# A delta rule's diagonal blocks, zeroed margins and decay buffer, moved within an eight-head software plan

## The chip, the cores and the metric

The kernel runs on one core of a Trainium2 chip. The metric is the device time of one execution in microseconds (us). The core has a matrix engine (TensorE, PE in the profile, with its weight loads as PEld), three engines for elementwise work (VectorE, DVE; ScalarE, ACT; GpSimd, POOL) and a queue that only issues transfers (SyncE, SP). Every engine works through its own queue in order. Engines wait for each other and for DMA transfers by semaphores.

## The reference

A decoder trunk of two layers over 1024 tokens of width 1024. Each layer projects the normalised input once, runs sparse attention and a gated delta rule side by side, gates and adds both, and projects back. The change touches the delta rule alone:

```python
qkv_b = jax.nn.silu(causal_depthwise_conv(qkv_b, conv_w[layer]))      # 4 taps, zeros ahead of the first token
q_b, k_b = l2_normalize(q_b), l2_normalize(k_b)
...
q, k, v = c4(q) * (dk ** -0.5), c4(k), c4(v)                          # chunks, 8 heads of 128
beta, gc = c3(beta), jnp.cumsum(c3(g), axis=-1)
decay = jnp.exp(jnp.where(incl, gc[..., :, None] - gc[..., None, :], -jnp.inf))
lower = jnp.where(strict, jnp.einsum('bhnid,bhnjd->bhnij', kb, k) * decay, 0.0)
tmat = jnp.eye(CHUNK) + lower
u = triangular_solve(tmat, v * beta[..., None]); w = triangular_solve(tmat, kb * jnp.exp(gc)[..., None])
q_dec = q * jnp.exp(gc)[..., None]
...
def step(state, xc):
    v_new = u_c - w_c @ state
    o_c = qd_c @ state + qk_c @ v_new
    state = state * gt_c + kd_c.T @ v_new
```

## The kernel before

Activations live as 128 partitions by tokens. Every projection in float32 is three matmuls of 128 x 512 (high times high, high times low, low times high, L388), 24 for one half of a feature tile and 48 for a whole one. A layer has a token phase (index scores, keys, values, selection), a feature phase (the delta rule), and an attention phase. The program is written with a framework whose scheduler fixes the order of each engine's queue when the program is built, by priority and by when it believes that inputs will be ready.

The feature phase (`feature_phase`, L673) runs over eight heads. For each head it projects and convolves keys, queries and values (`conv`, L736: 48 matmuls each). From the second head on it then projects the output gates of the head before (`gdn_finish`, L892: 96 matmuls). So a head takes 144 matmuls at first and 240 in steady state; the last head is followed by further gate projections.

In `conv`, ScalarE copies each accumulated half into a padded row `xp` (L748) and writes the last tap into `kf`, `qf` or `vv` (L749); VectorE adds three more taps of 128 x 1024 (L755); a tanh on ScalarE (L757) and one VectorE operation (L758) finish the activation. `xp` has two buffers in turn, and its four leading columns, the zeros ahead of the first token, are written once a layer by GpSimd (L682).

Everything else of a head is put between those projection matmuls by a plan. `plan_head` (L699) enters steps with a position, counted in projection matmuls from the head's own start; `planned` (L306) emits a step when the count reaches its position, with a priority far above the projections, and with an order on TensorE behind the matmul just emitted and on ScalarE behind the last evacuation (`issue_after`). For VectorE, GpSimd and SyncE a planned step has the priority alone, so there the scheduler may set it earlier. In order of position a head's steps are:

- 80, `decays_load` (L717): GpSimd issues a 512 KB load into `H` (two buffers), masks it (L723), and issues another of 512 KB (L727) with the queries' decays, `qe`. That tile shares its one buffer, "wide", with the tile `ln` of the inverse (L926). `decays_exp` (118): ScalarE turns `H` into decays (L734), queued behind the last evacuation.
- 100 and 106, `gdn_keys`: TensorE turns the keys (L765), ScalarE squares them (L771), VectorE sums (L772), makes `kdec` (L784), and runs the reciprocal root (`rsqrt`, L130) for the norms. 138, `gdn_row`: one row of scales goes out to memory and back as `ccomp`.
- 142 and 147, `gdn_queries`: the same squares for the queries.
- 151 to 163, `gdn_products`: products of keys with keys and queries (L831), multiplied by the decays on VectorE (L833, L834).
- 163, `gdn_inverse`: VectorE multiplies `qf` by `qe` (L838), then `inverse_blocks` (L917) writes the 32 x 32 diagonal blocks out (L925), reads them back as `ln` (L928), inverts them all by 31 steps on VectorE (L938, L940), writes the result out (L944) and reads it back into `H` (L947).
- 352 to 382, `inverse_pairs` (L949): VectorE turns three of the diagonal blocks into `XF` (L956), and TensorE joins blocks to 64 and to 128 (L965 to L992).
- 390 to 544, `gdn_chunks` (L852): 23 steps of the recurrence over eight chunks (L865 to L888), the last users of the head's `H`.
- 552, `norms` (L898): mean square and reciprocal root of the outputs on VectorE, ending in L903. 562 and 568, `outputs` (L905): TensorE turns the result (L909), VectorE gates it (L910).

In steady state, seen from the head whose keys are being projected, its predecessor's pairs lie at matmul 112 and after, and the norm and outputs of the one before that at 72, 82 and 88; the query projection ends at 96.

Of the kernel before, what the change touches and what calls it, by code (L numbers as in the profile page):

```python
# [20 lines left out]
try:  # L21
# [4 lines left out]
F32 = mybir.dt.float32  # L26
# [5 lines left out]
OP = mybir.AluOpType  # L32
# [4 lines left out]
P = 128  # L37
S = 1024
# [31 lines left out]

AT_DECAYS, AT_EXP, AT_KEYS, AT_ROW, AT_QUERIES, AT_PRODUCTS, AT_VALUES, AT_PAIRS, AT_CHUNKS, AT_NORMS, AT_OUTPUTS = (
    80, 118, (100, 106), 138, (142, 147), (151, 155, 159, 163), (204, 210), 352, 390, 552, (562, 568))

STEP_PAIRS, STEP_CHUNKS = 6, 7

# [1 line left out]
def ap(t, offset, dims):  # L79
    return bass.AP(tensor=t.tensor, offset=t.offset + offset, ap=dims)  # L80
# [13 lines left out]
class Trunk:  # L94
# [207 lines left out]
    def at(self, pos, step):  # L302

        self.plan.append((pos, len(self.plan), step))
# [368 lines left out]
    def feature_phase(self, l, ht):  # L673
        nc, tc = self.nc, self.tc
        self.yb = self.dram.tile([HEADS, P, S], F32, name="yb")
        with tc.tile_pool(name="feat", bufs=1) as p, self.banks(ch=(1, 2), oc=(1, 1), more=(1, 1)):
            XF = p.tile([P, T, 64], F32, name="xf")
            nc.gpsimd.memset(XF, 0.0)

            self.xps = [p.tile([P, S + 4], F32, name=f"xp{i}") for i in range(2)]  # L680
            for a in self.xps:
                nc.gpsimd.memset(a[:, 0:4], 0.0)  # L682
            self.count, hd = 0, None
            for h in range(HEADS + 1):
                before, hd = hd, None
                if h < HEADS:
                    hd = dict(h=h, at=self.count)
                    self.plan_head(p, hd, XF)
                    for name, base, bufs in (("kf", 1024, 3), ("qf", 0, 3), ("vv", 2048, 1)):
                        self.conv(l, p, ht, hd, name, base, bufs)  # L690
                if h >= HEADS - 1:
                    i = h - HEADS + 2
                    for f in range(sum(GATES[:i]), sum(GATES[:i + 1])):
                        self.gate_a(l, ht, f)
                if before:
                    self.gdn_finish(l, p, ht, before)
            self.planned()

    def plan_head(self, p, hd, XF):  # L699

        at = lambda pos, *steps, gap=0: [self.at(hd["at"] + pos + i * gap, f) for i, f in enumerate(steps)]
        at(AT_DECAYS, lambda: self.decays_load(p, hd))
        at(AT_EXP, lambda: self.decays_exp(hd))
        for half in range(2):
            at(AT_KEYS[half], lambda half=half: self.gdn_keys(p, hd, half))
            at(AT_QUERIES[half], lambda half=half: self.gdn_queries(hd, half))
            at(AT_VALUES[half], lambda half=half: self.gdn_values(p, hd, half))
        at(AT_ROW, lambda: self.gdn_row(p, hd))
        for i, pos in enumerate(AT_PRODUCTS):
            at(pos, lambda i=i: self.gdn_products(p, hd, 2 * i))  # L710
        at(AT_PRODUCTS[-1], lambda: self.gdn_inverse(p, hd))
        pairs = self.inverse_pairs(p, hd, XF)
        at(AT_PAIRS, *[lambda: next(pairs, None)] * 6, gap=STEP_PAIRS)
        chunks = self.gdn_chunks(p, hd)
        at(AT_CHUNKS, *[lambda: next(chunks, None)] * (3 * T - 1), gap=STEP_CHUNKS)

    def decays_load(self, p, hd):  # L717


        nc, h = self.nc, hd["h"]  # L720
        E = hd["H"] = p.tile([P, T, P], F32, name="H", bufs=2)
        nc.gpsimd.dma_start(out=E, in_=ap(self.rows, h * P, [[0, P], [8 * P, T], [1, P]]))
        masked = nc.gpsimd.affine_select(E, E, pattern=[[0, T], [1, P]], compare_op=OP.is_ge, fill=MASKED, base=0,  # L723
                                         channel_multiplier=-1)
        qe = hd["qe"] = p.tile([P, 32, 32], F32, name="wide", bufs=1).rearrange("p a b -> p (a b)")
        with self.tc.issue_after(masked.ins):
            nc.gpsimd.dma_start(out=qe.rearrange("p (t c) -> p t c", c=P),  # L727
                                in_=ap(self.rows, (T * 8 + h) * P, [[0, P], [8 * P, T], [1, P]]))
# [7 lines left out]
    def conv(self, l, p, ht, hd, name, base, bufs):  # L736

        nc = self.nc
        feat = self.feat[l]
        dst = hd[name] = p.tile([P, S], F32, name=name, bufs=bufs)  # L740
        col = base + hd["h"] * P
        cw = lambda j: feat[:, 24 * j + col // P:24 * j + col // P + 1]
        self.xps.append(self.xps.pop(0))
        xp = self.xps[0]

        def evac(hs, acc):
            o = hs.start
            nc.scalar.copy(xp[:, 4 + o:516 + o], acc)  # L748
            self.act_last = nc.scalar.activation(dst[:, hs], acc, AF.Copy, scale=cw(3)).ins  # L749

        ws = self.feat_weights(self.w_in[l], C_QKVB + col)
        for half in range(2):
            self.proj_feat(ws, half, ht, evac)
        for j in range(3):
            nc.vector.scalar_tensor_tensor(dst, xp[:, 1 + j:1 + j + S], cw(j), dst, op0=OP.mult, op1=OP.add)  # L755
        th = xp[:, 4:4 + S]
        nc.scalar.activation(th, dst, AF.Tanh, scale=0.5)  # L757
        nc.vector.scalar_tensor_tensor(dst, th, 1.0, dst, op0=OP.add, op1=OP.mult)  # L758
# [76 lines left out]

    def gdn_inverse(self, p, hd):

        self.nc.vector.tensor_mul(hd["qf"], hd["qf"], hd["qe"])  # L838
        with self.tc.high_priority(offset=AHEAD - PLANNED):
            self.inverse_blocks(p, hd["H"], hd["ccomp"])  # L840

# [107 lines left out]
    def inverse_pairs(self, p, hd, XF):  # L949

        nc, nc_ = self.nc, hd["nc"]
        XT = H = hd["H"]
        for b in range(3):
            bs = slice(32 * b, 32 * b + 32)
            co = 32 if b == 1 else 0
            nc.vector.transpose(XF[bs, :, co:co + 32], XT[bs, :, bs])  # L956
        yield
        ncb = lambda sl, n: nc_[sl, :, None].to_broadcast([sl.stop - sl.start, T, n])
        y2 = p.tile([P, T, 32], F32, name="y2", bufs=1)

        pairs = [(slice(32 * b, 32 * b + 32), slice(32 * b + 32, 32 * b + 64)) for b in (0, 2)]
        py = self.bank("ch")
        for c in range(T):
            for k, m in pairs:
                nc.tensor.matmul(py[m, 32 * c:32 * c + 32], H[k, c, m], XF[k, c, 0:32], start=True, stop=True)  # L965
        for k, m in pairs:
            nc.vector.tensor_mul(y2[m], py[m, :256].rearrange("p (c i) -> p c i", c=T), ncb(m, 32))
        yield
        pz = self.bank("ch")
        for c in range(T):  # L970
            for k, m in pairs:
                nc.tensor.matmul(pz[k, 32 * c:32 * c + 32], y2[m, c], XT[m, c, m], start=True, stop=True)
        for k, m in pairs:
            nc.scalar.copy(XT[k, :, m], pz[k, :256].rearrange("p (c i) -> p c i", c=T))
        yield
        m = slice(32, 64)
        pw = self.bank("ch")
        for c in range(T):
            nc.tensor.matmul(pw[m, 32 * c:32 * c + 32], XT[m, c, m], y2[m, c], start=True, stop=True)
        nc.scalar.copy(XF[m, :, 0:32], pw[m, :256].rearrange("p (c i) -> p c i", c=T))  # L980
        yield
        k, m = slice(0, 64), slice(64, 128)
        py = self.bank("ch")
        for c in range(T):
            nc.tensor.matmul(py[m, 64 * c:64 * c + 64], H[k, c, m], XF[k, c], start=True, stop=True)
        y3 = XF
        nc.vector.tensor_mul(y3[m], py[m].rearrange("p (c i) -> p c i", c=T), ncb(m, 64))
        yield
        pz = self.bank("ch")
        for c in range(T):  # L990
            nc.tensor.matmul(pz[k, 64 * c:64 * c + 64], y3[m, c], XT[m, c, m], start=True, stop=True)
        nc.scalar.copy(XT[k, :, m], pz[k].rearrange("p (c i) -> p c i", c=T))  # L992
# [252 lines left out]
```

## Time and profile before

| What | us |
|---|---|
| three runs, median (lowest to highest) | 2746.72 (2743.76 to 2749.48) |
| the profiled execution, its own time | 2755.04 |
| its span, first to last instruction | 2753.4 |
| granted TensorE clock, mean over the span | 0.974 |

How to read it: times are us from the span's start unless marked ns. A group's line gives source line, engine, operation, what it writes and reads, shapes and count. A row of the timeline gives start, duration, engine, line, operation, tiles, shape and count, and in brackets how long the engine sat idle before it and what ended that. A row of the waits gives who waited for whom: us in total, times, longest. The feature phase runs from about 365 to 1108 us in the first layer and from about 1740 to 2464 in the second.

### The profile page before, as it was taken

To read this page: it belongs to the slowest core of one execution; us is meant where nothing else is said; L and a number is where in the kernel's file an instruction comes from. 1 tells how busy PE (TensorE), PEld (TensorE's weight loads), DVE (VectorE), ACT (ScalarE), POOL (GpSimd) and SP (SyncE) were. 2 spreads that over 40 slices of the span, in tenths; PEclk is the share of its full clock that TensorE was granted. 3 is DMA by queue.
4 is the path that set the end of the run, shared out by engine and by line. 5 is a ranking of instruction groups with operands and counts; after the bars stand their busy time and mean duration, and the time that the engine had idled before them with its cause. 6 is when DMAs were issued, how large, how long until landed. Compare 5 with 4: busy or idle time off the path is not lost.

```text
span 2753.4 us, 42170 instructions
## 1 busy us (share of the span) xinstructions
PE 2595.2 (94%) x14858; PEld 2134.8 (78%) x14858; DVE 1886.2 (69%) x5082; ACT 1348.4 (49%) x3107; POOL 135.4 (5%) x386
## 2 busy tenths in 40 slices
PE   7999989989999999999999999899999999999998
PEld 7677767777777788898786777677778777888986
DVE  6678967666676663598356779676767666637965
ACT  5579634343333332598135796333434334237962
POOL 0122000000000000000001220000000000000000
PEclk9999999998999999999999999999999999999999
DMA  3123232142333322431411232321332323234223
GB/s 120 47 66 95 81 82 57 42 79 54 63 56 69 57 60 68 153 102 47 152 53 48 65 97 80 82 66 35 84 75 46 67 60 62 64 103 132 88 83 128
DMA packets 285431, 211.35 MB, mean 77 GB/s; under 512 B 72290, under 2 KB 239268, under 8 KB 285220
## 3 DMA queue, kind: packets, MB, share of 16 engines
q1 hardware_dynamic: 280612, 191.88, 24.8%
q0 software_dynamic: 4608, 16.78, 5.0%
q8 instruction: 117, 1.92, 0.3%
q14 instruction: 94, 0.77, 0.1%
HBM read 162.19 MB, written 46.40 MB: 76 GB/s over the span
## 4 chain that ended last, share of the span: by engine, by line
PE 56%; DVE 11%; DMA 7%; issue 3%; ACT 2%; SPq 1%; POOL 0%; DVEq 0%; ACTq 0%; POOLq 0%
PE acc L388 16%; PE more L388 7%; PE acc L365 7%; PE acc L1137 4%; PE wide L1105 4%; PE tr L1128 2%; DMA H<-xscr 2%; PE out L365 2%; DVE xtmp L938 2%; DVE xc L940 2%; PE tr L831 2%; PE out L388 2%; PE tr L765 1%; DVE w_lo L148 1%; DMA wide<-rows 1%
## 5 line engine op out<-in xcount | busy, mean ns | idle before, releaser
L388 PE MATMUL acc<-lo_t,w_hi 128*128 128x512 f32 x1240 | 511.4, 412 | 0.0
L388 PE MATMUL acc<-hi_t,w_hi 128*128 128x512 f32 x1240 | 503.2, 406 | 6.8 <-DVE gate L663 6.1
L388 PE MATMUL acc<-hi_t,w_lo 128*128 128x512 f32 x1240 | 503.7, 406 | 0.0
L147 ACT CAST w_hi<-w_raw 128x512 fp32r<-128x512 f32 (+1 forms) x336 | 201.4, 602 | 417.3 <-PE acc L388 214.6
L148 DVE TENSOR_TENSOR w_lo<-w_raw,w_hi 128x512 fp32r<-128x512 f32 (+1 forms) x336 | 223.7, 669 | 219.8 <-ACT w_hi L147 190.5
L365 PE MATMUL acc<-w_hi,hi_t 128*128 128x512 f32 (+1 forms) x768 | 287.5, 375 | 15.1 <-ACT w_hi L147 10.2
L365 PE MATMUL acc<-w_lo,hi_t 128*128 128x512 f32 (+1 forms) x768 | 286.8, 374 | 2.1 <-DVE w_lo L148 2.1
L365 PE MATMUL acc<-w_hi,lo_t 128*128 128x512 f32 (+1 forms) x768 | 285.2, 371 | 0.0
L388 PEld LDWEIGHTS acc<-hi_t,w_hi 128*128 128x128 f32 x1240 | 236.3, 191 | 57.2 <-DVE gate L663 7.5
L388 PEld LDWEIGHTS acc<-lo_t,w_hi 128*128 128x128 f32 x1240 | 236.8, 191 | 47.7
L388 PEld LDWEIGHTS acc<-hi_t,w_lo 128*128 128x128 f32 x1240 | 236.8, 191 | 45.3
L596 ACT ACTIVATE t_junk<-scores,t_bits 128x640 f16<-128x640 f32 x248 | 198.9, 802 | 29.5 <-DVE t_bits L588 24.7
L388 PE MATMUL more<-lo_t,w_hi 128*128 128x512 f32 x488 | 203.0, 416 | 0.0
L388 PE MATMUL more<-hi_t,w_hi 128*128 128x512 f32 x488 | 199.7, 409 | 1.7 <-ACT kf L749 1.7
L388 PE MATMUL more<-hi_t,w_lo 128*128 128x512 f32 x488 | 198.9, 408 | 0.0
L365 PEld LDWEIGHTS acc<-w_hi,hi_t 128*128 128x128 f32 x768 | 146.8, 192 | 45.6 <-ACT w_hi L147 13.9
L365 PEld LDWEIGHTS acc<-w_lo,hi_t 128*128 128x128 f32 x768 | 147.4, 192 | 28.5 <-DVE w_lo L148 5.3
L365 PEld LDWEIGHTS acc<-w_hi,lo_t 128*128 128x128 f32 x768 | 147.4, 192 | 22.8 <-issue 1.0
L578 DVE TENSOR_SCALAR_CACHE_REDUCE t_junk<-scores,t_bits 128x1024 f16<-128x1024 f32 (+4 forms) x136 | 153.5, 1128 | 4.3
L886 ACT COPY vb<-oc 128x128 f32<-128x128 f32 x128 | 34.1, 267 | 178.1 <-PE oc L885 169.8
L940 DVE TENSOR_TENSOR xc<-xc,xtmp 128x60 f32<-128x60 f32 (+24 forms) x496 | 104.9, 212 | 12.5
L938 DVE TENSOR_TENSOR xtmp<-wide,xc 128x60 f32<-128x60 f32 (+24 forms) x496 | 103.9, 210 | 12.4
(345 smaller groups left out, 5434.2 us busy)
## 6 DMA issues: line engine op xcount, KB each, us to landing
w_raw<-in_w_in_dram SPq DMA_DIRECT2D x272, 256.0 KB
qs<-stage SPq DMA_DIRECT2D x32, 256.0 KB
ya_gate<-gate SPq DMA_DIRECT2D x32, 256.0 KB
H<-rows POOLq DMA_DIRECT2D x16, 512.0 KB, 9.3
wide<-rows POOLq DMA_DIRECT2D x16, 512.0 KB, 7.6
wide<-hscr SPq DMA_DIRECT2D x64, 128.0 KB
yb<-gate SPq DMA_DIRECT2D x32, 256.0 KB
w_raw<-in_w_out_dram SPq DMA_DIRECT2D x32, 256.0 KB
```

The lines of the kernel that those rows point to most:

```text
L147: self.nc.scalar.copy(hi, src)
L148: self.nc.vector.tensor_sub(lo, src, hi.bitcast(F32))
L365: nc.tensor.matmul(acc[t][:, :n], a[:, k, ts], ws[k][b][:, :n], start=k == 0 and i == 0, stop=k == KT - 1 and i == 2)
L388: mm = self.nc.tensor.matmul(acc, ws[k // 4][a][:, cs], act[b][:, k, hs], start=k == 0 and i == 0, stop=k == KT - 1 and i == 2)
L578: nc.vector.tensor_scalar(junk[:, :sc[i].shape[1]], sc[i], thr, 0.0, op0=op, op1=OP.add, accum_out=cnt[:, i:i + 1])
L596: nc.scalar.activation(junk[:, :n], sc[i], AF.Sign, bias=f(bits, i), scale=-1.0, accum_out=cnt[:, i:i + 1])
L831: nc.tensor.matmul(pg[:, o0:o0 + P], kf[:, cs], a[:, cs], start=True, stop=True)
L938: nc.vector.tensor_mul(tmp[:, :n, j + 1:], ln[:, None, j, j + 1:].to_broadcast(shape), X[:, :n, j:j + 1].to_broadcast(shape))
L940: nc.vector.tensor_add(X[:, :n, j + 1:], X[:, :n, j + 1:], tmp[:, :n, j + 1:])
L1105: nc.tensor.matmul(ps[:, :w], qt[a][:, i], kt[b][:, g, o:o + w], start=j == 0, stop=j == 2)
L1128: nc.tensor.transpose(pt[:, o:o + P], rows[i][:, j * P:(j + 1) * P], self.ident)
L1137: nc.tensor.matmul(po, a, b[:, cs], start=j == 0 and i == 0, stop=j == t and i == 2)
```

## The change

Five things are altered. The three transposes that begin the pairs are ordered on VectorE behind the last convolution tap emitted so far; for most heads that is the next head's query convolution. The positions of pairs, chunks, norms and outputs grow by ten matmuls. The product of queries and decays becomes a step of its own at 184. `qe` gets its own buffer of 128 x 1024. The zero margins are written by VectorE.

```diff
-AT_DECAYS, AT_EXP, AT_KEYS, AT_ROW, AT_QUERIES, AT_PRODUCTS, AT_VALUES, AT_PAIRS, AT_CHUNKS, AT_NORMS, AT_OUTPUTS = (
-    80, 118, (100, 106), 138, (142, 147), (151, 155, 159, 163), (204, 210), 352, 390, 552, (562, 568))
+AT_DECAYS, AT_EXP, AT_KEYS, AT_ROW, AT_QUERIES, AT_PRODUCTS, AT_DECAYED, AT_VALUES, AT_PAIRS, AT_CHUNKS, AT_NORMS, AT_OUTPUTS = (
+    80, 118, (100, 106), 138, (142, 147), (151, 155, 159, 163), 184, (204, 210), 362, 400, 562, (572, 578))
...
             for a in self.xps:
-                nc.gpsimd.memset(a[:, 0:4], 0.0)
+                nc.vector.memset(a[:, 0:4], 0.0)
...
         at(AT_PRODUCTS[-1], lambda: self.gdn_inverse(p, hd))
+        at(AT_DECAYED, lambda: nc.vector.tensor_mul(hd["qf"], hd["qf"], hd["qe"]))
...
-        qe = hd["qe"] = p.tile([P, 32, 32], F32, name="wide", bufs=1).rearrange("p a b -> p (a b)")
+        qe = hd["qe"] = p.tile([P, S], F32, name="qe", bufs=1)
...
         for j in range(3):
-            nc.vector.scalar_tensor_tensor(dst, xp[:, 1 + j:1 + j + S], cw(j), dst, op0=OP.mult, op1=OP.add)
+            self.convolved = nc.vector.scalar_tensor_tensor(dst, xp[:, 1 + j:1 + j + S], cw(j), dst, op0=OP.mult,
+                                                            op1=OP.add).ins
...
     def gdn_inverse(self, p, hd):
 
-        self.nc.vector.tensor_mul(hd["qf"], hd["qf"], hd["qe"])
         with self.tc.high_priority(offset=AHEAD - PLANNED):
             self.inverse_blocks(p, hd["H"], hd["ccomp"])
...
-        for b in range(3):
-            bs = slice(32 * b, 32 * b + 32)
-            co = 32 if b == 1 else 0
-            nc.vector.transpose(XF[bs, :, co:co + 32], XT[bs, :, bs])
+        with self.tc.issue_after(self.convolved):
+            for b in range(3):
+                bs = slice(32 * b, 32 * b + 32)
+                co = 32 if b == 1 else 0
+                nc.vector.transpose(XF[bs, :, co:co + 32], XT[bs, :, bs])
```

More of the change, by code (lines that the diff above doesn't have):

```diff
@@ L699, in plan_head @@
     def plan_head(self, p, hd, XF):
+        nc = self.nc
         at = lambda pos, *steps, gap=0: [self.at(hd["at"] + pos + i * gap, f) for i, f in enumerate(steps)]
```

## The prediction

> **What bounds the kernel now.** I read the page first, then who waited for whom on TensorE, then the order of time around each long wait.
>
> ```profile
> span 2753.4 us, 42170 instructions
> ...
> PE 2595.2 (94%) x14858; PEld 2134.8 (78%) x14858; DVE 1886.2 (69%) x5082; ACT 1348.4 (49%) x3107; POOL 135.4 (5%) x386
> ```
>
> TensorE works for 94% of the span, so the matmul stream is the bound, and an edit that touches no matmul can only win TensorE's gaps. The list of TensorE's waits (who, for whom: us in total, times, longest) says which gaps this edit can reach:
>
> ```profile
> PE tr L909 <- DVE vb L903: 48.2, 12, 6.7
> PE tr L765 <- issue: 18.0, 2, 9.0
> ...
> PE ch L965 <- DVE xf L956: 10.7, 4, 4.8
> PE tr L831 <- DVE H L834: 10.2, 2, 5.2
> ...
> PE tr L909 <- DVE H L834: 2.8, 1, 2.8
> ```
>
> All five lie in the two feature phases. Idle time is not the whole price. The busy times of stretches that begin where TensorE starts again (stretch, its length, the engines, then granted TensorE clock, DMA share, GB/s) show a slow clock behind the waits. First and last of the eight long L909 waits, four a layer:
>
> ```profile
> 701.60:708.60 7.00, 7.00 (x26) 5.90 (x27) 4.21 (x6) 2.82 (x7) 0.00 (x0) 0.61 0.90 139
> ...
> 2315.10:2322.10 7.00, 7.00 (x33) 6.02 (x34) 4.53 (x7) 3.53 (x10) 0.00 (x0) 0.78 0.58 166
> ```
>
> Behind the two L765 waits:
>
> ```profile
> 398.90:405.90 7.00, 6.98 (x26) 5.92 (x27) 5.55 (x10) 3.90 (x6) 0.00 (x0) 0.69 0.00 0
> 1774.30:1781.30 7.00, 7.00 (x26) 5.92 (x27) 5.50 (x10) 3.85 (x6) 0.00 (x0) 0.68 0.01 2
> ```
>
> Behind three of the four L965 waits:
>
> ```profile
> 484.20:491.20 7.00, 7.00 (x93) 4.88 (x93) 1.59 (x4) 1.18 (x2) 0.00 (x0) 0.69 0.40 98
> 638.00:656.00 18.00, 17.96 (x140) 13.13 (x141) 3.46 (x7) 3.05 (x7) 0.00 (x0) 0.53 0.17 39
> 1856.70:1863.70 7.00, 6.99 (x94) 4.76 (x94) 1.61 (x4) 1.57 (x4) 0.00 (x0) 0.76 0.36 99
> ```
>
> Length times (1 - clock) is the time lost: 2.7 us behind the first L909 wait, 1.5 behind the last, about 2.0 each; 4.4 behind both L765 waits; 2.2 + 8.5 + 1.7 = 12.4 behind the L965 waits.
>
> **The change part by part.**
>
> *Transposes behind the taps.* VectorE's timeline before the first long L909 wait:
>
> ```profile
> 692.36 0.43 DVE L956 STREAM_TRANSPOSE xf<-H 32x256 f32<-32x256 f32 x1
> 692.82 0.17 DVE L140 TENSOR_TENSOR rs_t<-rs_y 128x8 f32<-128x8 f32 x1
> 698.48 0.44 DVE L956 STREAM_TRANSPOSE xf<-H 32x256 f32<-32x256 f32 x1 [5.50 <-DMA H<-xscr]
> ...
> 700.30 1.22 DVE L903 TENSOR_TENSOR vb<-vb,rs_y 128x1024 f32<-128x1024 f32 x1
> ```
>
> The third transpose (of the next head's inverse) stands in the middle of the norm's reciprocal root. It waits 5.5 us for its DMA, and the norm, the output transposes and TensorE wait behind it. The transposes do not shrink (48 of them, 0.43 us each); they move behind the next head's query taps, which come later than the output transposes. That is an order on one engine and no new semaphore: behind them in VectorE's queue stand the rest of the keys' reciprocal root and L967, and for XF itself only TensorE's L965 waits. Without them and the wait L903 would begin at 700.3 - 5.5 - 1.3 = 693.5 and end at 694.7, just ahead of the moment at which TensorE ran dry, 701.58 - 6.28 = 695.3. Norms and outputs move by the same ten matmuls, so this margin stays. Gain: 48.2 less about 1 for the small ones, plus 8 x 2.0 of clock: **63**.
>
> *Margins.* POOL, VectorE and TensorE at the start of the phase:
>
> ```profile
> 385.15 1.09 POOL L723 TENSOR_SCALAR_AFFINE_SELECT H<-H 128x1024 f32<-128x1024 f32 x1 [6.30 <-DMA H<-rows]
> ...
> 389.56 1.09 POOL L723 TENSOR_SCALAR_AFFINE_SELECT H<-H 128x1024 f32<-128x1024 f32 x1 [2.46 <-DMA H<-rows]
> 390.61 0.13 POOL L682 MEMSET xp<- 128x4 f32 x2
> ```
> ```profile
> 390.77 2.60 DVE L755 SCALAR_TENSOR_TENSOR kf<-xp,feat,kf 128x1024 f32<-128x1024 f32 x2 [9.30 <-POOL xp L682]
> ```
> ```profile
> 398.92 1.94 PE L765 MATMUL tr<-ident,kf 128*128 128x128 f32 x8 [9.04 <-issue]
> ```
>
> Two tiny memsets queue on POOL behind masks that wait for DMAs, and the first key taps wait 9.3 us for them. On VectorE a memset of 128x4 is not in the trace; bounds are nothing and POOL's 0.13 us for two, and I take 0.1, nearest to POOL's own. VectorE idled from 381.5 to 390.8, so it is hidden. The taps start 9.3 us earlier and cover TensorE's 9.0. Gain: 18.0 + 4.4 = **22**.
>
> *Own buffer, and the product of queries and decays moved to 184.* POOL, SP and VectorE:
>
> ```profile
> 470.38 0.91 POOL L727 DMA_DIRECT2D wide<-rows  x1 [79.64 <-DVE xc L940]
> ```
> ```profile
> 481.69 1.81 SPq L947 DMA_DIRECT2D H<-xscr  x4
> ```
> ```profile
> 570.56 1.23 DVE L838 TENSOR_TENSOR qf<-qf,wide 128x1024 f32<-128x1024 f32 x1 [4.58 <-DMA wide<-rows]
> ```
>
> While the heads start up, the decays' load waits for the end of the previous inverse (470.38) and then runs beside that inverse's way out, so the blocks come back late (481.69, 11 us behind) and L965 waits. With a buffer of its own the load is done long before. The 4.58 us before L838 (and the 2.8 of the L909 wait for L834 behind it) go too. The product still costs 1.23 us a head. Gain: 10.7 + 12.4, of which I strike half of the 8.5 us behind 638 because that stretch is full of small matmuls whose clock may stay low anyway: 18.9; with the 2.8, **22**. Against it: head 1's load, freed by head 0's product, now falls beside head 0's own inverse.
>
> ```profile
> wide<-rows POOLq DMA_DIRECT2D x16, 512.0 KB, 7.6
> ```
>
> That can cost the inverse between nothing and the load's own 7.6 us to landing; the blocks come back some 8 us earlier (what 481.69 stood behind) and TensorE asks 2.3 us later, so I take nothing. On SP no transfer changes place: the inverse's stores (L925) wait for the last L834, which no longer has L838's 1.23 us ahead of it, and so go out that much earlier. POOL loses the two memsets and the wait for the inverse, and its in-order queue issues nothing later than before.
>
> *Ten matmuls later* for pairs, chunks, norms, outputs. Full clock is 0.234 us a matmul, so 2.3 us. The last head's chunks end at its matmul 554 instead of 544, inside the 624 that its gates still bring: the tail hides it. But head i + 2 loads its H only when head i's chunks release the buffer. At the start that feeds the L831 waits (10.2 in two): I charge 2 x 2.3, **5**. In the steady heads:
>
> ```profile
> 687.53 0.89 POOL L722 DMA_DIRECT2D H<-rows  x1 [60.18 <-ACT g_u L872]
> 698.35 1.09 POOL L723 TENSOR_SCALAR_AFFINE_SELECT H<-H 128x1024 f32<-128x1024 f32 x1 [9.93 <-DMA H<-rows]
> ```
> ```profile
> 706.29 0.69 ACT L749 ACTIVATE qf<-acc,feat 128x512 f32<-128x512 f32 x1
> 706.87 0.40 ACT L734 ACTIVATE H<-H,ngm 128x128 f32<-128x128 f32 x1
> 707.76 0.60 ACT L771 ACTIVATE th<-tr 128x512 f32<-128x512 f32 x1 [0.49 <-PE tr L765]
> ```
>
> The mask ends at 699.44 and will end at 701.8. ScalarE reaches the exponentials at 706.87, but 6.28 + 2.7 of that was the wait that goes, and half an output (0.4) moves behind it: 697.5. So ScalarE will wait some 4.0 us there. The last steady head gives less (mask end 2310.9 + 2.3; exponentials 2320.2 - 6.7 - 1.5 - 0.4), 1.8:
>
> ```profile
> 2309.83 1.09 POOL L723 TENSOR_SCALAR_AFFINE_SELECT H<-H 128x1024 f32<-128x1024 f32 x1 [8.36 <-DMA H<-rows]
> ```
> ```profile
> 2320.16 0.40 ACT L734 ACTIVATE H<-H,ngm 128x128 f32<-128x128 f32 x1
> ```
>
> Behind the exponentials stand the squares of the keys (L771), on which VectorE waits between two taps.
>
> *What is late next.* VectorE's taps and TensorE's first pair product:
>
> ```profile
> 707.02 1.28 DVE L755 SCALAR_TENSOR_TENSOR qf<-xp,feat,qf 128x1024 f32<-128x1024 f32 x1 [0.38 <-ACT qf L749]
> ...
> 711.50 1.28 DVE L755 SCALAR_TENSOR_TENSOR qf<-xp,feat,qf 128x1024 f32<-128x1024 f32 x1
> ...
> 713.03 0.42 DVE L967 TENSOR_TENSOR y<-ch,g_nc 32x256 f32<-32x256 f32 x1 [0.17 <-PE ch L965]
> ...
> 714.23 1.28 DVE L755 SCALAR_TENSOR_TENSOR qf<-xp,feat,qf 128x1024 f32<-128x1024 f32 x1
> ```
> ```profile
> 712.29 0.69 PE L965 MATMUL ch<-xf,H 32*32 32x32 f32 x32
> ```
>
> The last tap ends at 715.5, 3.2 us behind TensorE's first use of XF, and three transposes add 1.3: 4.5 late. Ten matmuls and the half output give 2.7 back, and the two L967 (0.9 with its gap 1.1) now come after: 0.7 left. ScalarE's wait adds itself less the 0.5 that L771 already waited: 1.3 to 3.5. So L965 waits 2.0 to 4.2 us in each of eight heads; I take 2.6, below the middle, as the 4.0 is one head's and the rows near the other end are more. Would the clock drop too? A wait of this size:
>
> ```profile
> 1856.71 0.22 PE L965 MATMUL ch<-xf,H 32*32 32x32 f32 x2 [1.94 <-DVE xf L956]
> ```
>
> It was followed by clock 0.76, 1.7 us lost. I charge half of that, 0.9, since a wait need not fall so. New waits: 8 x 3.5 = **28**.
>
> The Trainium skill (TensorE: Matmul & The Clock Gate, "Part 1: The HAM clock gate") lets the clock fall only after an idle window of about 3.4 us. By it the new waits would cost no clock and the sum would be 7 us better; the 0.76 behind a gap of 1.94 us speaks against it here, so the trace's charge stays.
>
> **Sum.** Gains 63 + 22 + 22 = 107; charges 28 + 5 = 33; net **-74**. The profiled execution took 2755.0 us (1.6 around its span), so it would take 2681. The median of the three runs, 2746.7, is 8.3 lower, and the gaps are taken to be the same there: **2673**.
>
> **The rivals.**
> 1. *Nothing new is late*: the scheduler sets L965 far enough behind the taps. For it: 0.7 us of lateness without ScalarE's wait. Against: the row at 698.35. 2747 - 107 = 2640. Chance 0.25.
> 2. *The taps are much later*: planned steps outrank them on VectorE (two of the keys' steps already split them), and with waits beside them L965 loses 7.5 us a head: 107 - 60 - 5 = 42, 2705. For it: taps 707.02 to 715.5 for 3.9 us of work. Chance 0.18.
> 3. *Slower*: same place, but XF so late that the wait passes 107 / 8 = 13.4 us a head with its clock; then the pairs, and the chunks behind them, are where the time is lost. At 15 us: 2760. Against: VectorE idles often in this stretch. Chance 0.05.
> 4. *It does not do what it says*: the scheduler may still put the memsets or transposes behind something that waits, for instance the memset where its memory is not yet free, or a transpose ahead of its DMA. With the norms' 63 and the new waits both absent: 2747 - 44 + 5 = 2708. Chance 0.05.
>
> The forecast has 0.47. The range, 2636 to 2710, takes in rivals 1, 2 and 4 and leaves out 3 and the edges of 1 and 2. About 0.2% (5.5 us) is what a measurement of this kernel can tell from no change: faster 0.94, same 0.02, slower 0.04.
>
> **What would show it.** Right: L909 no longer waits for L903, and VectorE's wait of L956 for H<-xscr is gone; L765 does not wait at the phase's start; L965 does not wait for the first heads, and waits 2 to 4 us in four heads a layer with ScalarE's L734 waiting for POOL just before. Wrong: L909 waits still stand with another name behind them, or L965 waits beyond 5 us. If the clock stays below 0.8 in stretches without a gap, the some 30 us of clock in the gains were not the gaps' doing.

## The result, and the profile after

The changed kernel took 2669.92 us (median of 4 runs, 2667.03 to 2674.24) beside 2748.10 for the kernel before on the same chip (4 runs): a ratio of 0.9716, 95% interval 0.9692 to 0.9739, or 78 us less. Its profiled execution took 2668.25 us. Lines of the changed kernel stand two or three further down than those of the kernel before (L956 is now L959, L965 L968, L765 L768, L831 L834, L903 L905, L909 L911, L723 L725, L734 L736, L771 L774), and the experiments share the new numbers, but for undo_buffer (one less between its two edits, so L767 for L768) and load_after_blocks (three more).

The page's head, after:

```profile
span 2666.4 us, 42133 instructions
...
PE 2565.7 (96%) x14858; PEld 2115.4 (79%) x14858; DVE 1893.6 (71%) x5086; ACT 1349.6 (51%) x3107; POOL 136.1 (5%) x382
```

TensorE runs the same 14858 matmuls. The two profiled executions lie further apart than the medians, since that of the kernel before took 2755.04 us, 7 above its median: the span lost 87.0 us. TensorE's idle time (span less busy) fell from 2753.4 - 2595.2 = 158.2 to 2666.4 - 2565.7 = 100.7, so 57.5, and its busy time by the other 29.5, the same matmuls at a higher clock (0.974 to 0.988 over the span). I use this split, idle and busy, for every run below; it belongs to the profiled execution, not to the median.

TensorE's waits after (us in total, times, longest):

```profile
PE ch L968 <- DVE rs_t L140: 14.9, 8, 3.5
...
PE ch L878 <- ACT g_u L874: 9.9, 2, 5.0
...
PE tr L768 <- issue: 1.4, 2, 0.7
...
PE tr L911 <- DVE vb L905: 0.4, 2, 0.2
...
PE tr L911 <- DVE H L837: 0.2, 1, 0.2
```

Of the five waits that the prediction read, four are gone: the norm's 48.2 is 0.4, the phase start's 18.0 is 1.4, the start-up waits of the pairs are gone, and 2.8 is 0.2. The 10.2 of L831 only changed its name: two gaps of 5 us stand behind L878 now, and in the first of them VectorE still waits 4.00 us for the exponentials of head 2's `H`. The new row is the first one: L968, eight times, one in each steady head. The name "rs_t L140" is that of an instruction of the keys' root which VectorE runs between the transposes; what TensorE needs is `XF`. ScalarE, VectorE and TensorE around the first of the eight:

```profile
672.22 0.69 ACT L751 ACTIVATE qf<-acc,feat 128x512 f32<-128x512 f32 x1
674.79 1.57 ACT L736 ACTIVATE H<-H,ngm 128x128 f32<-128x128 f32 x5 [1.88 <-POOL H L725]
676.27 0.58 ACT L774 ACTIVATE th<-tr 128x512 f32<-128x512 f32 x1
```
```profile
673.80 2.04 DVE L757 SCALAR_TENSOR_TENSOR qf<-xp,feat,qf 128x1024 f32<-128x1024 f32 x1
676.88 0.69 DVE L775 TENSOR_REDUCE g_ssq<-th 128x4 f32<-128x512 f32 x1 [1.04 <-ACT th L774]
...
680.82 1.28 DVE L757 SCALAR_TENSOR_TENSOR qf<-xp,feat,qf 128x1024 f32<-128x1024 f32 x1
682.02 0.17 DVE L138 TENSOR_SCALAR g_rk<-g_rk 128x8 int32<-128x8 int32 x1
682.10 0.43 DVE L959 STREAM_TRANSPOSE xf<-H 32x256 f32<-32x256 f32 x1
```
```profile
682.67 0.21 PE L968 MATMUL ch<-xf,H 32*32 32x32 f32 x2 [1.72 <-DVE rs_t L140]
```

This is the chain that the prediction drew: the exponentials wait 1.88 us for the mask, the squares stand behind them in ScalarE's queue, VectorE idles 1.04 us for the squares between two taps, the last tap ends at 682.1, the transposes follow it, and TensorE has been dry for 1.72 us.

### The profile page after: what moved, and what is told of

Its sections match the earlier page's. It is cut to its first block, busy times and chain, and to the rows that moved or that the text cites. A ratio compares the mean times of both kernels' runs of the same rounds, so it can differ in the third digit from the quotient of the medians.

```text
span 2666.4 us, 42133 instructions
## 1 busy us (share of the span) xinstructions
PE 2565.7 (96%) x14858; PEld 2115.4 (79%) x14858; DVE 1893.6 (71%) x5086; ACT 1349.6 (51%) x3107; POOL 136.1 (5%) x382
## 4 chain that ended last, share of the span: by engine, by line
PE 46%; issue 20%; DVE 6%; DMA 4%; ACT 3%; POOL 1%; SPq 0%; DVEq 0%; POOLq 0%; ACTq 0%
PE acc L388 12%; PE acc L365 7%; PE more L388 5%; PE acc L1140 4%; PE wide L1108 4%; PE tr L1131 2%; PE out L365 2%; PE out L388 2%; PE tr L834 1%; ACT t_junk L596 1%; DMA H<-rows 1%; DVE t_junk L578 1%; PE wide L545 1%; DMA w_raw<-in_w_out_dram 1%; DVE scores L554 1%
## 5 line engine op out<-in xcount | busy, mean ns | idle before, releaser
L388 PE MATMUL acc<-lo_t,w_hi 128*128 128x512 f32 x1240 | 502.9, 406 | 0.0
L596 ACT ACTIVATE t_junk<-scores,t_bits 128x640 f16<-128x640 f32 x248 | 198.9, 802 | 30.4 <-DVE t_bits L588 25.6
L365 PEld LDWEIGHTS acc<-w_hi,hi_t 128*128 128x128 f32 x768 | 146.7, 191 | 43.5 <-ACT w_hi L147 13.0
L874 ACT COPY g_u<-ch 128x128 f32<-128x128 f32 x128 | 33.9, 267 | 163.8 <-PE ch L872 163.6
```

The costliest lines, as they stand in the source:

```text
L365: nc.tensor.matmul(acc[t][:, :n], a[:, k, ts], ws[k][b][:, :n], start=k == 0 and i == 0, stop=k == KT - 1 and i == 2)
L388: mm = self.nc.tensor.matmul(acc, ws[k // 4][a][:, cs], act[b][:, k, hs], start=k == 0 and i == 0, stop=k == KT - 1 and i == 2)
L596: nc.scalar.activation(junk[:, :n], sc[i], AF.Sign, bias=f(bits, i), scale=-1.0, accum_out=cnt[:, i:i + 1])
L874: nc.scalar.copy(u, pu)
```

## The experiments

Each changes the changed kernel in a few places. "Idle" and "busy" are TensorE's, from the page of the profiled execution.

| Kernel | median us | ratio to before, 95% | idle | busy |
|---|---|---|---|---|
| before | 2748.10 | 1 | 158.2 | 2595.2 |
| the change | 2669.92 | 0.9716 (0.9692 to 0.9739) | 100.7 | 2565.7 |
| again: the change once more | 2678.10 | 0.9749 (0.9736 to 0.9763) | 101.1 | 2568.3 |
| undo_margins | 2710.77 | 0.9866 (0.9848 to 0.9884) | 120.7 | 2592.4 |
| undo_buffer | 2694.78 | 0.9813 (0.9799 to 0.9826) | 108.8 | 2583.8 |
| undo_order | 2660.05 | 0.9682 (0.9668 to 0.9697) | 95.1 | 2566.0 |
| undo_shift | 2640.36 | 0.9608 (0.9590 to 0.9627) | 83.8 | 2550.9 |
| no_order_no_shift | 2703.37 | 0.9840 (0.9820 to 0.9860) | 131.3 | 2575.2 |
| exp_later | 2647.52 | 0.9639 (0.9619 to 0.9659) | 82.9 | 2562.9 |
| no_order_exp_later | 2643.15 | 0.9626 (0.9605 to 0.9647) | 82.1 | 2557.9 |
| load_after_blocks | 2652.61 | 0.9651 (0.9625 to 0.9677) | 89.6 | 2562.8 |
| order_exp_later | 2641.04 | 0.9609 (0.9583 to 0.9636) | 79.9 | 2559.4 |
| order_first_chunks | 2636.55 | 0.9599 (0.9574 to 0.9625) | 81.2 | 2561.8 |
| order_both | 2651.43 | 0.9652 (0.9628 to 0.9676) | 80.0 | 2568.2 |

The runs from again to undo_order shared one occasion and its chip, those from undo_shift to no_order_exp_later a second, the last four a third; the kernel before gave 2746.63, 2748.73 and 2748.93 us there (9 runs each). Ratios carry across, medians of us nearly so.

**again.** No edit.

> The changed kernel, nothing altered, so that the kernels of this group stand beside it on one chip. Both theories: 2670 us where before takes 2748 (ratio 0.972).

It came out 8 us above the first measurement; the intervals meet. So a difference of some 8 us between two occasions means nothing, and effects are compared with this run where they share its occasion.

**undo_margins.**

```diff
-                nc.vector.memset(a[:, 0:4], 0.0)
+                nc.gpsimd.memset(a[:, 0:4], 0.0)
```

> The changed kernel with the two margin memsets back on GpSimd. Theory (each part took away its own wait, and the gains add): the first keys' taps wait about 9 us in each layer again, TensorE idles 16 to 18 us in the two L768 waits, and with the clock behind them (4.4) the time is 20 to 22 us longer, about 2691. Rival (the start of the phase is hidden by something later, such as head 2's wait for H): within 5 us of 2670.

The old wait is back in full, in its waits:

```profile
PE ch L968 <- DVE rs_t L140: 19.0, 8, 3.7
PE tr L768 <- issue: 17.8, 2, 9.4
```

That is 17.8 - 1.4 = 16.4 us more idle, as the prediction had it. But the kernel lost 33 us against the repeat (2710.8 - 2678.1), more than the 20 to 22 expected. The profiled executions of the two lie 43.5 us apart (2714.75 and 2671.21, the longest time of the one and the shortest of the other): 19.6 us of it are idle and 24.1 busy. Little of the busy time stands behind the margins' own two waits: the stretch behind the first (first row below) lost 7 x 0.23 = 1.6 us, the one behind the second, at 0.67, 2.3. More of it stands behind the L968 waits, here the first two, 2.78 and 1.73 us long (stretch, length, engines, then granted clock, DMA share, GB/s):

```profile
401.00:408.00 7.00, 7.00 (x28) 5.99 (x29) 5.51 (x10) 4.09 (x7) 0.00 (x0) 0.77 0.00 0
...
698.57:705.57 7.00, 7.00 (x72) 4.71 (x74) 5.13 (x18) 1.20 (x2) 0.00 (x0) 0.57 0.47 130
779.42:786.42 7.00, 7.00 (x48) 4.52 (x49) 5.14 (x18) 1.21 (x2) 0.00 (x0) 0.52 0.11 23
```

These two run at about half clock, and so do the stretches behind the other six (0.50 to 0.59): 25.6 us are lost behind all eight. Behind the same eight waits the changed kernel lost 4.9 us in its first profile and 14.6 in the repeat. So the L968 waits account for 11 of the 24.1 us and the margins' own for 3.9; the other 9 are open. At the margins' own waits, then, stand 16.4 + 3.9 = 20 us, as forecast; the rest of the 33 is in part clock behind other waits.

**undo_buffer.** `qe` shares "wide" again, and the product stands in `gdn_inverse`.

```diff
-        at(AT_DECAYED, lambda: nc.vector.tensor_mul(hd["qf"], hd["qf"], hd["qe"]))
...
-        qe = hd["qe"] = p.tile([P, S], F32, name="qe", bufs=1)
+        qe = hd["qe"] = p.tile([P, 32, 32], F32, name="wide", bufs=1).rearrange("p a b -> p (a b)")
...
+        self.nc.vector.tensor_mul(hd["qf"], hd["qf"], hd["qe"])
```

> The changed kernel with the queries' decays back in the inverse's buffer and the product back ahead of the inverse. Theory: in the first three heads of a layer VectorE waits for the decays' load again and TensorE waits at the pairs, some 15 to 22 us, about 2690. Rival (the ten matmuls hide the late load): within 5 us of 2670, with the load still late in the trace but no TensorE wait behind it.

Its waits:

```profile
PE ch L968 <- DVE rs_t L140: 16.1, 8, 3.0
...
PE ch L968 <- DVE xf L959: 10.0, 4, 5.3
```

The four start-up waits are back with 10.0 us (10.7 before), and the kernel takes 17 us more than the repeat (the profiled executions lie 23 us apart, 7.7 idle and 15.5 busy; the prediction's term was 22). At the first of them GpSimd's load waits for the inverse, and starts with the inverse's stores:

```profile
458.02 0.91 POOL L728 DMA_DIRECT2D wide<-rows  x1 [67.81 <-DVE xc L942]
```
```profile
457.96 2.92 SPq L946 DMA_DIRECT2D xscr<-xc  x4
...
469.96 1.86 SPq L949 DMA_DIRECT2D H<-xscr  x4
```

The stores go out at 457.96 and the read-back is only issued at 469.96, 12 us later, where the changed kernel takes 462.69 - 458.69 = 4.0 at the same place. This is a small transfer beside a load of 512 KB, which the next runs meet again.

**undo_order.**

```diff
-        with self.tc.issue_after(self.convolved):
+        if True:
```

> The changed kernel without the order of the transposes behind the taps; the ten matmuls stay. Theory: the transposes stand in the norm's reciprocal root again and wait for their transfer, TensorE waits 40 us or more for the norm in eight heads, and the new wait of the pairs (14.9 us in eight) goes: 63 less some 20, so about 2710. Rival (the ten matmuls alone are enough, since the transfer has landed by then): the norm waits stay under 8 us and the time is at most 2670.

This expectation fell, and its rival held. Without the order the norm's wait did not come back, and the kernel is faster than the repeat by 18 us (2678.1 - 2660.1), with intervals apart. Its waits have no L968:

```profile
PE ch L975 <- DVE y L970: 9.9, 12, 1.8
...
PE tr L911 <- DVE vb L905: 3.2, 8, 0.8
```

VectorE shows why (start, duration; the transposes, then the beginning of the norm):

```profile
663.33 1.28 DVE L757 SCALAR_TENSOR_TENSOR kf<-xp,feat,kf 128x1024 f32<-128x1024 f32 x1
664.52 1.36 DVE L959 STREAM_TRANSPOSE xf<-H 32x256 f32<-32x256 f32 x3
...
667.28 0.17 DVE L903 SCALAR_TENSOR_TENSOR g_ms<-g_osq,g_zq 128x8 f32<-128x8 f32 x1
```

All three transposes run ahead of the norm and wait for nothing here; their blocks have come back. So the wait for H<-xscr itself, which the prediction took as given, was all but gone: 4.4 us over all heads, for 44.6 in the kernel before.

**undo_shift.** The order stays, and the ten matmuls go.

```diff
-    80, 118, (100, 106), 138, (142, 147), (151, 155, 159, 163), 184, (204, 210), 362, 400, 562, (572, 578))
+    80, 118, (100, 106), 138, (142, 147), (151, 155, 159, 163), 184, (204, 210), 352, 390, 552, (562, 568))
```

> The changed kernel with the old positions of pairs, chunks, norms and outputs; the order behind the taps stays. Theory A (the order behind the taps keeps the norm free by itself, the ten matmuls only give TensorE time): no norm waits, L968 waits longer, by up to 2.3 us in eight heads, so 2678 to 2700 where the changed kernel takes 2670 to 2678. Theory B (what frees the norm is that the load of H starts ten matmuls later and no longer runs beside the blocks' way back, H<-xscr): the two transfers run beside each other again, the blocks land about 10 us after their issue instead of 3, but since the transposes come after the taps it does no harm; the same time as by A. The two differ in when the transposes' input lands, not in the time.

Both theories missed the time: it is 30 to 38 us better than the change, at 0.9608. Its waits for the norm and the pairs are all but gone:

```profile
PE tr L834 <- DVE H L837: 10.9, 2, 5.6
...
PE tr L911 <- DVE vb L905: 1.1, 4, 0.3
PE ch L968 <- DVE xf L959: 0.5, 1, 0.5
```

The mask starts at 669.09 in place of 673.66, ScalarE's exponentials wait 0.63 us in place of 1.88, and the transposes run at 676.80, so that TensorE waits 0.50 us for them in this head and in no other. The prediction charged 28 + 5 us for the lateness in all; beside the order, the ten matmuls bring that much.

The expectation's two theories differ in when the blocks land, and the trace has that too, as the times at which the four read-backs of a head signalled their end: in each of the eight heads the last came 9.2 to 11.4 us after SP issued the first (issued 658.05, landed 669.42 in this one, with the load of the next `H` issued at 658.19). In the change it takes 3.2 to 3.7 us in seven of eight. So theory B has the landing right: the blocks are as late as ever here, and the order alone keeps that from the norm.

**no_order_no_shift.** Both of these edits together; what stays of the change is margins, buffer and the separate product.

> Only the margins, the buffer and the separate product; no order behind the taps and the old positions. Theory B (the collision of H<-rows with H<-xscr makes the wait of the transposes, and either the order or the ten matmuls removes it): L959 waits 3 to 6 us for H<-xscr in eight heads again and TensorE 30 to 48 us for the norm; with the margins' and buffer's gains the time is 2695 to 2715. Rival C (the buffer and the later product free the norm, by starting the inverse 1.2 us earlier): norm waits under 8 us and at most 2665.

The norm's wait is back, as large as ever:

```profile
PE tr L911 <- DVE vb L905: 48.9, 12, 7.2
```

The time and the wait are theory B's, and rival C falls. So either edit, the order or the ten matmuls, takes the wait away, and both are not needed. The order is worth 2703.4 - 2640.4 = 63 us here, where the ten matmuls are absent. VectorE, GpSimd and SP in the first steady head show what the wait is made of:

```profile
670.81 0.44 DVE L959 STREAM_TRANSPOSE xf<-H 32x256 f32<-32x256 f32 x1 [5.67 <-DMA H<-xscr]
```
```profile
659.68 0.88 POOL L724 DMA_DIRECT2D H<-rows  x1 [66.66 <-ACT g_u L874]
670.70 1.09 POOL L725 TENSOR_SCALAR_AFFINE_SELECT H<-H 128x1024 f32<-128x1024 f32 x1 [10.14 <-DMA H<-rows]
```
```profile
659.54 1.83 SPq L949 DMA_DIRECT2D H<-xscr  x4
```

The read-back of the blocks (SP, 659.54) and the load of a later head's decays (GpSimd, 659.68) are issued within 0.2 us of each other, and both are done within 0.2 us: the mask starts at 670.70, the transpose at 670.81. In six of the other seven heads the load goes out between 2.3 us ahead of the read-back and 0.2 behind it; in the last it is 9.5 us ahead. In the change and in undo_order, the ten matmuls hold the last user of `H` back, and so the load: in this head it goes out 3.5 us behind the read-back (665.03 for 661.52 in undo_order), which is then home (last landing at 664.79). That is a theory of a collision; load_after_blocks tests it alone.

**exp_later.** On the changed kernel, the exponentials are entered six matmuls later, behind the squares of the keys.

```diff
-    80, 118, (100, 106), 138, (142, 147), (151, 155, 159, 163), 184, (204, 210), 362, 400, 562, (572, 578))
+    80, 124, (100, 106), 138, (142, 147), (151, 155, 159, 163), 184, (204, 210), 362, 400, 562, (572, 578))
```

> The changed kernel with the exponentials of H at 124 instead of 118, which puts them on ScalarE behind the first half of the values' evacuation and so behind the keys' squares. Theory D (L968 waits because the squares stand behind the exponentials, which wait for the mask): ScalarE's wait of 1.9 us ahead of the squares goes, the last tap ends 1 to 2 us earlier, the L968 waits fall from 15 to 18 us to under 6, and the time is 10 to 20 us below the changed kernel's. Rival (the taps and the transposes fill VectorE by themselves): L968 still waits over 12 us and the time is within 5 us of the changed kernel's.

ScalarE now does the squares first, and TensorE's wait at the pairs has all but gone:

```profile
672.15 0.60 ACT L774 ACTIVATE th<-tr 128x512 f32<-128x512 f32 x1 [1.11 <-PE tr L768]
673.75 0.60 ACT L774 ACTIVATE th<-tr 128x512 f32<-128x512 f32 x1 [1.01 <-PE tr L768]
...
678.09 2.45 ACT L736 ACTIVATE H<-H,ngm 128x128 f32<-128x128 f32 x8
```
```profile
PE ch L968 <- DVE rs_t L140: 1.4, 3, 0.5
```

It gains 22 to 31 us on the change (0.9639), more than the 10 to 20 expected. So the new wait did come from the exponentials standing ahead of the squares, one engine further up than the profile names.

**no_order_exp_later.** exp_later without the order.

> The changed kernel without the order behind the taps and with the exponentials at 124. Theory B and D together: no norm waits (under 8 us in all), no L968 waits, the L975 waits for L970 (9.9 us without the order) fall below 5 as the taps end earlier; 2645 to 2655, below every kernel so far. Rival: with the order gone the exponentials are on no path that TensorE waits for, and the time is that of the kernel without the order, 2660.

0.9626: the same as exp_later, 2 us under the expected range, and undo_shift stays as fast. No wait for L968 or L970 is left in its list, and 2.6 us for the norm. Once the squares are in time, the order costs nothing, and gains nothing either.

**load_after_blocks.** The collision by itself: no order, the old positions, but the load of `H` is held until the transposes have read the blocks (GpSimd copies one column of `XF` and issues the load behind that). So that the exponentials do not hold the squares, they stand at 124.

```diff
-    80, 118, (100, 106), 138, (142, 147), (151, 155, 159, 163), 184, (204, 210), 362, 400, 562, (572, 578))
+    114, 124, (100, 106), 138, (142, 147), (151, 155, 159, 163), 184, (204, 210), 352, 390, 552, (562, 568))
...
-        nc.gpsimd.dma_start(out=E, in_=ap(self.rows, h * P, [[0, P], [8 * P, T], [1, P]]))
+        turned = self.small.tile([P, 1], F32, name="g_turned")
+        read = nc.gpsimd.tensor_copy(turned, XF[:, 0, 0:1])
+        with self.tc.issue_after(read.ins):
+            nc.gpsimd.dma_start(out=E, in_=ap(self.rows, h * P, [[0, P], [8 * P, T], [1, P]]))
...
-        with self.tc.issue_after(self.convolved):
+        if True:
```

> Margins, buffer and separate product only, with no order behind the taps and the old positions (2703 us, norm waits 48.9), and now the load of H waits on GpSimd until the transposes of the head before are done (a copy of one column of XF stands ahead of it), so that it can't run beside H<-xscr; its exponentials move to 124. The transposes keep their place inside the norm's reciprocal root. Theory B (the collision makes their wait): the wait of the transposes for H<-xscr falls from 40.7 to under 15 us and the norm waits from 48.9 to under 15; 2640 to 2665. Rival (the way back takes its 10 us by itself, as its pieces are small): both waits stay within 10 us of 40.7 and 48.9; 2690 to 2715.

VectorE and GpSimd in the same place (lines three further down):

```profile
665.53 0.43 DVE L962 STREAM_TRANSPOSE xf<-H 32x256 f32<-32x256 f32 x1 [0.60 <-DMA H<-xscr]
...
667.11 0.44 DVE L962 STREAM_TRANSPOSE xf<-H 32x256 f32<-32x256 f32 x1
```
```profile
667.68 1.16 POOL L725 COPY g_turned<-xf 128x1 f32<-128x1 f32 x1 [50.98 <-DVE xf L962]
668.78 0.88 POOL L727 DMA_DIRECT2D H<-rows  x1
```

The transposes still stand in the middle of the norm's root, as before the change, but the blocks are back 3.6 us after SP issued the read-back (661.93), where no_order_no_shift needed 11.3. In all eight heads the last block lands 3.1 to 4.1 us after the first is issued. VectorE's wait for H<-xscr falls from 40.7 us (8 times) to 0.6 (once), TensorE's wait for the norm from 48.9 to 4.6, the time from 2703 to 2653. The later exponentials are in this run too, but they stand behind the norm, and order_exp_later, next, shows that they bring nothing where the squares are in time. Holding the load has a price as well: TensorE waits 15.7 us in four places for L840, the products with the decays, where no_order_no_shift waited 10.7 in two. So the collision is the cause; where the transposes stand in the queue only decides who pays for it.

**order_exp_later, order_first_chunks, order_both.** undo_shift again, with the exponentials at 124, with the first head's chunks six matmuls apart in place of seven (to free its `H` sooner for the two L834 waits), and with both.

```diff
-        at(AT_CHUNKS, *[lambda: next(chunks, None)] * (3 * T - 1), gap=STEP_CHUNKS)
+        at(AT_CHUNKS, *[lambda: next(chunks, None)] * (3 * T - 1), gap=STEP_CHUNKS - (hd["h"] == 0))
```

> The changed kernel with the old positions (2640 us) and the exponentials of H at 124. Theory D: with the old positions the mask is done when the exponentials come (ScalarE waits 0.6 us), so there is little left to win: 2632 to 2640. Rival (the two gains add, as they stand on different waits): 2610 to 2620.

> The changed kernel with the old positions, and the chunk steps of head 0 six matmuls apart instead of seven, so that head 0 gives back its H 22 matmuls (5 us) earlier. Theory (the two L834 waits of 5.6 us are head 2 waiting for that buffer): they fall from 10.9 to under 4 us, and with their clock the time is 8 to 14 us below 2640. Rival (head 0's chain of chunks is bound by its own latency at the start): the waits stay and TensorE waits inside the chain.

> The changed kernel with the old positions, exponentials at 124 and head 0's chunk steps six apart. If the last two kernels' gains are of different waits they add: 2622 to 2632; if one takes the other's, the lower of the two.

The first, 0.9609, is undo_shift's 0.9608: nothing left to gain there. The second, 0.9599, is 4 us under 2640 in place of the 8 to 14 expected. The L834 waits are gone from its list, and a new row has come, 7.0 us for 10.9:

```profile
PE ch L872 <- DVE g_r L869: 7.0, 2, 3.6
```

It is the same wait under another name. VectorE and TensorE at the first of the two:

```profile
536.14 0.42 DVE L836 TENSOR_TENSOR A<-tr,H 128x256 f32<-128x256 f32 x1 [4.28 <-ACT H L736]
536.48 0.34 DVE L869 SCALAR_TENSOR_TENSOR g_r<-ch,g_nce,vb 128x128 f32<-128x128 f32 x1
```
```profile
536.88 0.79 PE L872 MATMUL ch<-g_r,H 128*128 128x128 f32 x2 [3.57 <-DVE g_r L869]
```

The load of head 2's `H` does go out earlier (525.74 for 532.53 in undo_shift), but still too late: VectorE stands at the product of head 2, waiting for the exponentials, ScalarE for the mask, and the step of the chunks that TensorE needs is queued on VectorE behind that product. So the theory has the right buffer, but the gain did not come; TensorE does wait inside the chain, as the rival has it, but not for the chain's own latency. Both edits together miss their expectation and are worse than either, 0.9652, with as little idle time as the best but 2568.2 busy; why is open. A third buffer for `H`, which would cut this wait at its root, was not tried. The three best, 0.960 to 0.961, can't be told apart, and all beat the change by some 30 us.

## Why the prediction was right, and where its working was not

The time (78 us less for 74 forecast) and the direction came out, and most steps did. The forecast's idle terms make 47.2 + 18.0 + 10.7 + 2.8 - 5 - 8 x 2.6 = 53, against 57.5 measured; its clock terms make 16 + 4.4 + 8.2 - 8 x 0.9 = 21, against 29.5 of busy time, both in the profiled executions, which lie 87 us apart. A few of its sums are off without moving the forecast: 701.8 - 697.5 is 4.3, not 4.0, the last head's 2313.2 - 2311.6 is 1.6, not 1.8, and the prices of rivals 1 and 3 leave out the charge of 5.

*Margins.* Right. The memsets stand at 374.61 with 0.10 us for both, the estimate's value, and the wait was worth 16.4 us of idle time. Undoing it cost 33 for the forecast's 22: about 20 at the wait itself, and more behind other waits.

*Own buffer and later product.* Right; 17 us measured by undoing it, for 22. Head 1's load beside head 0's inverse cost nothing to be seen, as taken.

*Ten matmuls later, for head 2's H.* The charge of 5 was not seen: 10.2 us before and 9.9 after, under another name.

*What is late next.* Right in its mechanism, mis-sized a little. L968 waited in each of the eight steady heads, with ScalarE's wait for the mask before it: 14.9 us in all, 17.9 in the repeat, for 8 x 2.6 = 20.8. The heads were the wrong way round: the forecast gave ScalarE 4.0 us in the first and 1.8 in the last, and it waited 1.65 to 1.88 in seven and 3.66 in the last. There the load still goes out beside the read-back (2217.73 and 2217.19), and the mask is late with it. The clock behind the eight waits cost 4.9 us in one execution and 14.6 in the other, for 7.2. exp_later showed the cause. Rival 1 (nothing late, 2640) is what the kernel would have been without the ten matmuls: undo_shift gave 2640.

*Transposes behind the taps.* The order does what this step says, at its price: from no_order_no_shift to undo_shift, which differ in the order alone, TensorE's wait for the norm falls from 48.9 to 1.1 us and the time by 63 us, the term as it stands. What the step missed is why the blocks were 5.5 us late, and that the ten matmuls cure the same wait. The four kernels side by side (median us and ratio):

| | old positions | ten matmuls later |
|---|---|---|
| no order | 2703.4 (0.9840) | 2660.1 (0.9682) |
| the order | 2640.4 (0.9608) | 2669.9 and 2678.1 (0.9716, 0.9749) |

The prediction counted the ten matmuls as a charge only. Beside the order they are one, 30 to 38 us for the 33 that it put down; alone they win some 43, by moving the load off the read-back. And in the change, where the blocks are in time already, the order takes nothing away and costs 10 to 18 us by itself, as it puts the transposes behind taps that are late. What the prediction overlooked stood in two rows that it quoted: the third transpose started at 698.48 after its DMA, the mask at 698.35 after its own. Two transfers that end together may be one event. SP of the kernel before shows that they also began together:

```profile
687.38 1.83 SPq L947 DMA_DIRECT2D H<-xscr  x4
```

against 687.53 for H<-rows. The forecast came out because the two edits overlap, and it counted their common gain once and the cost of both; that one of them was better left out it did not see.

*The Trainium skill's clock rule* (TensorE: Matmul & The Clock Gate, "Part 1: The HAM clock gate"), by which the new waits would cost no clock: six of the change's L968 waits, of 1.49 to 1.72 us, cost none, and a seventh of 1.67 was followed by a clock of 0.54 for 7 us. In this case an idle gap below the rule's window can be cheap, but is not safe.

## What to carry to other kernels

When an engine waits for a DMA, look what else was released at the same moment, and then when both transfers were issued: moving one of them may do as much as re-queuing the instruction that waits. When a change has two edits that could each cure the same wait, undo each by itself and both together, as one of them may be pure cost. On engines that work in order, follow a wait further than the profile names, here from the transposes over the taps and the squares to an exponential that waited for a mask.

## What was not expected of the hardware

*The clock behind short waits.* The eight L968 waits of the changed kernel; first three rows of the second layer, and the stretches of 7 us behind the last two of them:

```profile
1996.72 0.22 PE L968 MATMUL ch<-xf,H 32*32 32x32 f32 x2 [1.65 <-DVE rs_t L140]
2074.84 0.22 PE L968 MATMUL ch<-xf,H 32*32 32x32 f32 x2 [1.63 <-DVE rs_t L140]
2153.02 0.22 PE L968 MATMUL ch<-xf,H 32*32 32x32 f32 x2 [1.67 <-DVE rs_t L140]
```
```profile
2074.84:2081.84 7.00, 7.00 (x103) 4.95 (x103) 5.44 (x19) 3.23 (x8) 0.00 (x0) 1.00 0.16 40
2153.02:2160.02 7.00, 7.00 (x63) 4.57 (x66) 5.13 (x18) 1.21 (x2) 0.00 (x0) 0.54 0.14 34
```

Waits of 1.63 and 1.67 us in the same code were followed by full clock and by 0.54. The eight together lost 3.2 + 1.7 us of clock in these stretches (1.7 behind the last, 3.49 us long), for the 7 charged; the same eight lost 14.6 in the repeat, where nothing was altered, and 25.6 in undo_margins. What decides it is not known from these runs; a price per wait is an average at best.

*A small transfer beside a large one.* The read-back is four transfers of 32 KB. Over the steady heads of the kernel before, the change, undo_order, undo_shift, no_order_no_shift and load_after_blocks, the last of them landed 3.1 to 4.1 us after the first was issued where the 512 KB load on GpSimd's queue came 1.3 us or more behind it, 8.2 to 11.5 us after where the load was issued between 2.3 us ahead and 0.9 behind, and 7.2 in the two heads where it was 9.5 ahead. Where the load came just behind the first read-back (0.13 to 0.19 us), the first two landed in time (2.0 to 2.4 us each) and the other two took 8.5 to 10.4. Why the small transfers are held until about the large one's end is not shown.

*VectorE beside GpSimd's mask.* A query tap of 128 x 1024 takes 1.28 us; the one that runs at 673.80, while the mask runs at 673.66, took 2.04. By the lines of the taps:

```profile
L757 DVE SCALAR_TENSOR_TENSOR qf<-xp,feat,qf x48: 1270/1279/2114, 384.0 to 2235.5; 128x1024 f32<-128x1024 f32 x48
```

(ns, least, median, most). In the kernel before the most was 1286; now the later mask falls beside a tap. It costs nothing at this place, since VectorE waits 1.04 us for the squares right after.
